# Seven products for eight on more K tiles of a chain of projections, and a feed forward in four parts

## The chip, the cores and the metric

The kernel runs on one core of a Trainium2 chip, in one launch. The metric is the device time of that core in microseconds, lower is better.

## The reference

Three layers on 256 tokens of width 2048, all in float32: two hybrid layers (chunked band attention, gated linear attention, attention to a memory, output projection, layer norm) and one block with a recurrent mixer, a forgetting attention, gates and a feed forward. What the change touches are dense products of the third block:

```python
proj = h @ w_in                        # its gate columns g_a and g_b, 2048 each
merged = jax.nn.sigmoid(g_a) * y_a + jax.nn.sigmoid(g_b) * y_b
x = x + rms_norm(merged @ w_o, norm_mix_post)
h = rms_norm(x, norm_ffn_pre)
gate, up = jnp.split(h @ w_ffn_in, 2, axis=-1)          # 5632 columns each
x = x + rms_norm((jax.nn.silu(gate) * up) @ w_ffn_down, norm_ffn_post)
```

## The kernel before

The kernel is a list of jobs. A job multiplies 256 tokens (two halves of 128) by 512 columns of a weight, over K tiles of 128 rows. Weights come from HBM in tiles of 512 KB (two K tiles by 512 columns) on SyncE's queue. Each is split into two float32r parts, a high one on ScalarE and the rest on VectorE (lines 356, 357, and 506, 507 for the shared jobs), and `three` (lines 439 to 443) multiplies with three matmuls of 512 columns: high by high, high by low, low by high. A tile of weights ("part") so costs 12 matmuls, for both halves of the tokens. All scratch is 41 slots of 512 KB (`N_SLOT`), for raw weights, split weights, hidden rows and sums alike.

`run` walks over the parts in order. `ahead` (line 370) loads up to four raw tiles and splits up to `N_HL` = 6 parts in front of the one that TensorE is told to run, as far as slots are free. Work of other stages (attention heads, recurrence, hidden groups) waits in generators that `pump` steps when they are due by an estimated clock, or that a consumer drains.

`Shared` (line 79) is two jobs with the same activations, a (gate) and b (up). For a quad of four K tiles they form a product of 2 by 2 blocks on each side: the two halves of the tokens by the two pairs of K tiles, and the two pairs of K tiles by the two jobs. Eight block products would be needed; seven do, with sums of blocks as operands (c, d, a, T1, T2, T3 and T4, each with 6 matmuls). Sums of the activations are made once per quad (`combos_of`, line 616, on GpSimd and VectorE). Sums of the weights are made in place for every pair by accumulating transfers between slots, which GpSimd issues (`add`, line 303; `sums`, line 317): after the split of "a" it issues a += b, b += d and d += a, and after that of "c" it issues c += d. T1 is the split of a, T2 of d, T3 of b and T4 of c, as they then stand. TensorE runs plain parts, d and c first, then a, T1, T2, T4, T3 into four PSUM banks and the two main tiles; ScalarE and VectorE combine them (lines 462 and 483 to 497).

In the feed forward (from line 1784) 11 groups of 512 hidden columns are done in parts of 4, 4 and 3. The first group is two single jobs; the other ten are shared pairs with one quad, K tiles 12 to 15. After a part's groups come four single jobs for `w_ffn_down`, whose sums over the parts are kept in four slots (`post_part`, line 1768; `residual_jobs`, line 1614, for the last part and for `w_o`). `hidden` (line 1742) turns a finished pair into the rows that the down jobs read; a job that needs them earlier drains it (line 1760).

Of the kernel before, what the change touches and what calls it, by code (L numbers as in the profile page):

```python
# [12 lines left out]
ALU = mybir.AluOpType  # L13
# [45 lines left out]
class Job:  # L59
# [72 lines left out]
class Builder:  # L132
# [116 lines left out]
    def run(self, jobs, loaded_first, split_first):  # L249
# [283 lines left out]
def network(ctx, tc, a):  # L533
# [82 lines left out]
    def combos_of(get2, quad):  # L616

        xi, ci = B.alloc(2)
        x, c = v4(xi), s(ci).rearrange("p (n k t) -> p n k t", n=4, k=2)
        for k in (0, 2):  # L620
            both = get2(quad[k])
            G.tensor_tensor(x[:, k:k + 2], both[:, :, 0, :].bitcast(F32), both[:, :, 1, :].bitcast(F32), ALU.add)
        x11, x21, x12, x22 = (x[:, k:k + 2, t * P:t * P + P] for k in (0, 2) for t in (0, 1))
        G.tensor_tensor(c[:, 0], x22, x21, ALU.subtract)
        G.tensor_tensor(c[:, 2], x11, x21, ALU.subtract)
        V.scalar_tensor_tensor(c[:, 1], c[:, 0], -1.0, x11, ALU.mult, ALU.subtract)
        G.tensor_tensor(c[:, 3], x12, c[:, 1], ALU.add)
        ids = B.alloc(2, F32R)
        B.split_to(s(ids[0]), s(ids[1]), s(ci))
        B.release([xi, ci])  # L630
        return ids

    def parted(ids):
        return tuple(s(i).rearrange("p (n k t) -> p n k t", n=4, k=2) for i in ids)
# [849 lines left out]

    def start_f(g):
        B.drain([gens["bf"]])
        st[f"yb{g}"] = B.alloc(2, F32R)
        fm = s(st["fm"])

# [37 lines left out]
    def post_gate(key, c):  # L1527
# [4 lines left out]
                A.activation(vt(st[f"{key}{c}"])[:, t, :], ps[:, t, :], AF.Tanh, scale=rs2h[:, t:t + 1])  # L1532
        return post

    def post_upb(c):
# [29 lines left out]

    merging = {}

    def merged(c):
# [4 lines left out]
        B.release([st[f"gb{c}"]])  # L1573

    def merged_get(kt):
        gen = merging.pop(kt // 4, None)
# [6 lines left out]
    for g in range(2):  # L1583
# [10 lines left out]
            X(6144 + 512 * g, 512, act, keep_rows(st, f"bv{g}"))  # L1594
        W(5120 + 512 * g, act, keep_scaled(st, f"bk{g}"))
        W(4096 + 512 * g, act, keep_scaled(st, f"bq{g}", SCALE, then=lambda g=g: start_f(g)))
    for c in range(4):
        X(9224 + 512 * c, 512, act, post_gate("gb", c))
# [4 lines left out]
    for c in range(3):  # L1603
        X(7176 + 512 * c, 512, act, post_gate("ga", c))
    for g in range(2):
        W(3072 + 512 * g, act, post_ag(g))
    X(7176 + 512 * 3, 512, act, post_gate("ga", 3))
# [3 lines left out]
                        pre=B.settle if c == 0 else None))  # L1611


    def residual_jobs(label, w_, post_row, resid, done, act_, order, k0=0, partial=None, pre1=None):

        q = {}

# [29 lines left out]
        def finish(t):  # L1647
# [9 lines left out]
        for c in range(4):  # L1657
            jobs.append(Job("x", w_, 512 * c, 512, act_, post(c), order=order, k0=k0,
                            pre={0: begin, 1: pre1, 2: load_x}.get(c), apart=(label, n - 4 if c == 2 else 0, n) if c > 1 else None))

    fact = row_act(lambda: B.release(xsrc["ids"]))
    f = {"h": []}
# [1 line left out]
    def mix_done(ids, t):  # L1664
        if t == 0:
            xsrc["ids"] = B.alloc(4)

        def rows(c):
            return vt(ids[c])[:, t, :]

        for c in range(4):
            eng = V if c % 2 == 0 else G
            eng.tensor_tensor(vt(xsrc["ids"][c])[:, t, :], rows(c), f["wb"](c), ALU.mult)

        f[t] = rows
        if t == 0:
            B.start(feeder(fact, 0, F0, FG))
        else:
            def done():
                B.release(ids + f["wi"])  # L1680
                f["make"] = make_fcombos()
                B.start(f["make"])
            start_late(fact, [f[0], f[1]], x1res, None, done, False)

    def pre_w2():
# [1 line left out]
        f["wb"] = bcast(a["norm_ffn_pre_2"][0], f["wi"])  # L1687

    residual_jobs("o", a["w_o_2"][0], a["norm_mix_post_2"][0], tokens(xres), mix_done, Act(merged_get), range(NKT),
                  pre1=pre_w2)  # L1690


    wf = a["w_ffn_in_2"][0]
# [23 lines left out]
            B.start(f[("gen", c)])  # L1717
        return post

    QUADS = [(12, 13, 14, 15)]  # L1720

    def make_fcombos():
        for quad in QUADS:
            f.setdefault("combos", []).append(combos_of(lambda k: B.act[:, k:k + 2], quad))
            yield 3000

    def fcombos(q):
        if f["make"] in B.side:
            B.drain([f["make"]])
        return parted(f["combos"][q])  # L1730

    def post_both(c):

        def post(gi, ui):
# [1 line left out]
            B.start(f[("gen", c)])  # L1736
            f["units"] = f.get("units", 1) + 1
            if f["units"] * 512 == D_FF:
                B.release(sum(f["combos"], []))
        return post  # L1740

    def hidden(c, gi, ui=None):
# [15 lines left out]
        B.release([gi])  # L1758

    def hidden_get(kt):  # L1760
        gen = f.pop(("gen", kt // 4), None)
# [3 lines left out]

    hact = Act(hidden_get)

    def post_part(c, new):
        def post(ps):
            if c == 0 and new:  # L1770
                f["part"] = B.alloc(4)
            p = s(f["part"][c])
            if new:
                V.tensor_copy(p, flat(ps))
            else:
                V.tensor_tensor(p, p, flat(ps), ALU.add)
        return post

    def out_done(ids, t):
        for c in range(4):  # L1780
# [1 line left out]
            eng.dma_start(a["out"][0, t * P:(t + 1) * P, c * 512:(c + 1) * 512], vt(ids[c])[:, t, :])  # L1782

    at = 0
    for g, n in enumerate((4, 4, 3)):
        for c in range(n):
            c0 = 512 * (at + c)
            head = (g, c) == (0, 0)
            if not head:
                std = range(16 - 4 * len(QUADS))  # L1790
                gate = Job("x", wf, c0, 512, fact, lambda ps: None, order=std, open=(1,))
                up = Job("x", wf, D_FF + c0, 512, fact, lambda ps: None, order=std)
                jobs.append(Shared(gate, up, QUADS, fact, fcombos, post_both(c)))
                continue
            jobs.append(Job("x", wf, c0, 512, fact, first_gate if head else post_gate2, apart=("ffn", 0, 8) if head else None))
            jobs.append(Job("x", wf, D_FF + c0, 512, fact, first_up if head else post_up2(c), apart=("ffn", 0, 4) if head else None))
        order, k0 = range(4 * n), 4 * at
        if g < 2:
            for c in range(4):
                jobs.append(Job("x", a["w_ffn_down_2"][0], 512 * c, 512, hact, post_part(c, g == 0), order=order, k0=k0))  # L1800
        else:
            residual_jobs("down", a["w_ffn_down_2"][0], a["norm_ffn_post_2"][0], tokens(x1res), out_done, hact, order, k0,
                          partial=lambda: f["part"])
        at += n

    B.run(jobs, load_b, lambda: (split_b(), B.release([mem_in.pop(0)])))
# [52 lines left out]
```

## Time and profile before

| | |
|---|---|
| median of 3 runs | 2400.83 us (2399.18 to 2401.85) |
| profiled execution | 2401.03 us; span from first to last instruction 2399.3 us |
| TensorE busy | 2380.5 us, 99% of the span |
| VectorE, ScalarE, GpSimd busy | 65%, 48%, 18% |
| granted TensorE clock, mean | 0.998 |
| accumulating transfers | 40 of 512 KB, median 7.2 us from issue to landing |

A busy share is that of the whole span; which engine a stretch waits for is read from the timelines of that stretch. A matmul's own duration in the trace overlaps with the next one's, so the price of one is the distance between starts.

### The profile page before, as it was taken

The numbers are of one execution on the slowest core, as the hardware profiler recorded it, in microseconds if no ns is written. First come the engines' busy times: TensorE is split into PE (matmuls) and PEld (weight loads), VectorE is DVE, ScalarE is ACT, GpSimd is POOL, SyncE is SP. The second block draws the span as 40 slices with busy tenths as digits, with TensorE's granted clock in tenths as the row PEclk, the third lists the DMA queues.
The fourth block names the chain that finished last, engine by engine and source line by source line (L and its number), as shares of the span: only waits on it lengthen the run. The fifth ranks groups of instructions, "written<-read, shape, count | busy, mean of one in ns | idle before, by whom it ended". The sixth has DMA issues, their size and how long they took to land. (4 is left out here: it accounts for less than half of the span.)

```text
span 2399.3 us, 31682 instructions
## 1 busy us (share of the span) xinstructions
PE 2380.5 (99%) x12045; PEld 2005.0 (84%) x12045; DVE 1566.2 (65%) x1783; ACT 1160.0 (48%) x1553; POOL 441.5 (18%) x646
## 2 busy tenths in 40 slices
PE   9999999999999999999999999999999999999998
PEld 7888888888888888888888888888888888888876
DVE  6587567566865667766775655657567557665675
ACT  5444455345454553655554434445555445544553
POOL 0330010004400110354754440001100000000000
PEclk9999999999999999999999999999999999999999
DMA  9545567674556574944654556675877578767773
GB/s 329 184 147 187 167 188 261 205 244 141 176 167 187 189 256 148 295 154 128 193 160 151 199 185 193 196 243 171 274 229 224 190 209 261 228 215 226 223 241 131
DMA packets 319672, 485.62 MB, mean 202 GB/s; under 512 B 22600, under 2 KB 162208, under 8 KB 319520
## 3 DMA queue, kind: packets, MB, share of 16 engines
q1 hardware_dynamic: 312528, 459.48, 58.8%
q0 software_dynamic: 6400, 23.07, 4.9%
q8 instruction: 94, 1.54, 0.3%
q10 hardware_dynamic: 592, 1.06, 0.1%
q14 instruction: 58, 0.48, 0.1%
HBM read 454.18 MB, written 8.40 MB: 193 GB/s over the span
## 5 line engine op out<-in xcount | busy, mean ns | idle before, releaser
L357 DVE TENSOR_TENSOR slot<-slot,slot 128x1024 fp32r<-128x1024 f32 x770 | 967.0, 1292 | 266.6 <-ACT slot L356 253.0
L356 ACT CAST slot<-slot 128x1024 fp32r<-128x1024 f32 x770 | 774.4, 1047 | 299.8 <-PE main L442 94.5
L428 PE MATMUL main<-act,slot 128*128 128x512 f32 x1824 | 651.2, 400 | 0.0
L441 PE MATMUL main<-slot,act 128*128 128x512 f32 x1488 | 589.5, 396 | 0.7 <-ACT slot L356 0.7
L442 PE MATMUL main<-slot,act 128*128 128x512 f32 x1488 | 580.0, 390 | 1.6 <-DVE slot L357 1.6
L443 PE MATMUL main<-slot,act 128*128 128x512 f32 x1488 | 580.3, 390 | 0.0
L429 PE MATMUL main<-act,slot 128*128 128x256 f32 x1824 | 510.0, 280 | 0.0
L428 PEld LDWEIGHTS main<-act,slot 128*128 128x128 f32 x1824 | 342.5, 188 | 80.3 <-issue 1.1
L429 PEld LDWEIGHTS main<-act,slot 128*128 128x128 f32 x1824 | 344.2, 189 | 0.8
L443 PEld LDWEIGHTS main<-slot,act 128*128 128x128 f32 x1488 | 279.3, 188 | 59.2
L442 PEld LDWEIGHTS main<-slot,act 128*128 128x128 f32 x1488 | 279.7, 188 | 58.3 <-DVE slot L357 2.8
L441 PEld LDWEIGHTS main<-slot,act 128*128 128x128 f32 x1488 | 279.6, 188 | 57.3 <-ACT slot L356 1.1
L441 PE MATMUL main<-slot,slot 128*128 128x512 f32 x620 | 244.2, 394 | 0.7 <-ACT slot L506 0.7
L443 PE MATMUL main<-slot,slot 128*128 128x512 f32 x620 | 242.6, 391 | 0.0
L442 PE MATMUL main<-slot,slot 128*128 128x512 f32 x620 | 242.1, 390 | 0.0
L304 POOL DMA_DIRECT2D slot<-slot x40 | 35.0, 874 | 563.4 <-DMA slot<-in_w_ffn_in_dram 196.8
L443 PEld LDWEIGHTS main<-slot,slot 128*128 128x128 f32 x620 | 116.8, 188 | 25.8 <-DVE slot L507 1.3
L441 PEld LDWEIGHTS main<-slot,slot 128*128 128x128 f32 x620 | 116.9, 188 | 25.3 <-ACT slot L506 1.4
L442 PEld LDWEIGHTS main<-slot,slot 128*128 128x128 f32 x620 | 116.8, 188 | 23.4
L507 DVE TENSOR_TENSOR slot<-slot,slot 128x1024 fp32r<-128x1024 f32 (+1 forms) x91 | 98.6, 1102 | 33.5 <-ACT slot L506 33.5
L846 POOL TENSOR_TENSOR slot<-slot 128x128 f32<-128x128 f32 x144 | 79.2, 581 | 192.3 <-PE main L428 93.2
L506 ACT CAST slot<-slot 128x1024 fp32r<-128x1024 f32 (+1 forms) x91 | 85.1, 956 | 47.0 <-DMA slot<-slot 16.5
(225 smaller groups left out, 1987.0 us busy)
## 6 DMA issues: line engine op xcount, KB each, us to landing
slot<-in_w_in_dram SPq DMA_DIRECT2D x384, 512.0 KB, 3.8
slot<-in_w_ffn_in_dram SPq DMA_DIRECT2D x176, 512.0 KB, 4.9
slot<-in_w_ffn_down_dram SPq DMA_DIRECT2D x88, 512.0 KB, 4.8
slot<-in_w_out_dram SPq DMA_DIRECT2D x64, 512.0 KB, 4.8
slot<-slot POOLq DMA_DIRECT2D x40, 512.0 KB, 7.2
slot<-in_w_o_dram SPq DMA_DIRECT2D x32, 512.0 KB, 4.7
slot<-in_w_mem_kv_dram SPq DMA_DIRECT2D x31, 512.0 KB, 6.4
slot<-in_w_up_b_dram SPq DMA_DIRECT2D x16, 512.0 KB, 4.6
```

The source lines that it names most:

```text
L304: nc.gpsimd.dma_start(self.s(out), self.s(x), accum_op=ALU.add)
L356: nc.scalar.copy(h, src)
L357: nc.vector.tensor_tensor(l, src, h.bitcast(F32), ALU.subtract)
L428: nc.tensor.matmul(job.ps[:, f, :], h[:, k, fs], xs, start=st, stop=False)
L429: nc.tensor.matmul(job.ps[:, f, :S], l[:, k, fs], xh, start=False, stop=en)
L441: nc.tensor.matmul(o, xh, h, start=start, stop=False)
L442: nc.tensor.matmul(o, xh, l, start=False, stop=False)
L443: nc.tensor.matmul(o, xl, h, start=False, stop=stop)
L506: nc.scalar.copy(h, src)
L507: nc.vector.tensor_tensor(l, src, h.bitcast(F32), ALU.subtract)
L846: G.tensor_tensor(view(E[:, l, :]), view(bt), ref, ALU.subtract)
```

## The change

Seven products for eight are used on more K tiles. Gate and up pairs have two quads, K tiles 8 to 11 and 12 to 15, where they had one. The down jobs of all parts but the last become two shared pairs each, with the first four K tiles of the part as a quad. The output projection's first two jobs become a pair with one quad, the last two stay. Of the eight gate jobs, four become two pairs with one quad. The last part's first two down jobs run interleaved, without a quad.

The feed forward runs in parts of 3, 3, 3 and 2 groups. In `Shared.sequence` the last two plain parts of both jobs move behind c, and a pair with two quads has one part less of look-ahead (`tight`). A class `Combos` makes the activations' sums in a generator, started when their rows are there.

```diff
-        self.apart, self.open = apart or (None, 0, 0), open
+        self.apart, self.open, self.tight = apart or (None, 0, 0), open, 0
...
-        rest = slice(2, None)
-        seq = own(self.b, slice(0, 1)) + mine("d") + own(self.b, slice(1, 2)) + mine("a") + own(self.b, rest)
-        seq += own(self.a, slice(0, 1)) + mine("c") + own(self.a, slice(1, None))
+        seq = own(self.b, slice(0, 1)) + mine("d") + own(self.b, slice(1, 2)) + mine("a") + own(self.b, slice(2, -2))
+        seq += own(self.a, slice(0, 1)) + mine("c") + own(self.a, slice(1, -2))
+        seq += own(self.b, slice(-2, None)) + own(self.a, slice(-2, None))
...
+        for x in (self, a, b):
+            x.tight = int(len(self.quads) > 1)
...
+            cap -= job.tight
             cap += sum(parts[j][0].kind == "s" and parts[j][1][0] == "a" for j in hls)
...
+    class Combos:
+        def start(self):
+            def gen():
+                for quad in self.quads:
+                    self.ids.append(combos_of(self.get2, quad))
+                    yield 3000
...
+    def shared_pair(w_, cs, act_, order, combos, post, pres=(None, None), k0=0):
+        std = [k for k in order if k not in sum(combos.quads, ())]
+        ja, jb = (Job("x", w_, c, 512, act_, lambda ps: None, order=std, k0=k0, pre=pre, open=op)
+                  for c, pre, op in zip(cs, pres, ((1,), ())))
+        return Shared(ja, jb, combos.quads, act_, combos, post)
...
+    jobs.append(shared_pair(w, (9224 + 512 * 2, 9224 + 512 * 3), act, range(NKT), gcombos, post_gates("gb", 2, False)))
...
+    jobs.append(shared_pair(w, (7176 + 512 * 0, 7176 + 512 * 1), act, range(NKT), gcombos, post_gates("ga", 0, True)))
...
+        if combos:
+            jobs.append(shared_pair(w_, (0, 512), act_, order, combos, both, (pre1, begin), k0))
+        else:
+            one, two = (Job("x", w_, 512 * c, 512, act_, post(c), order=order, k0=k0, pre=pre)
+                        for c, pre in ((0, pre1), (1, begin)))
+            jobs.append(Shared(one, two, [], act_, None, None))
...
-    QUADS = [(12, 13, 14, 15)]
...
+    fcombos = Combos(lambda k: B.act[:, k:k + 2], (8, 9, 10, 11), (12, 13, 14, 15))
...
-    for g, n in enumerate((4, 4, 3)):
+    for g, n in enumerate((3, 3, 3, 2)):
...
-        if g < 2:
-            for c in range(4):
-                jobs.append(Job("x", a["w_ffn_down_2"][0], 512 * c, 512, hact, post_part(c, g == 0), order=order, k0=k0))
+        if g < 3:
+            for c in (0, 2):
+                jobs.append(shared_pair(a["w_ffn_down_2"][0], (512 * c, 512 * c + 512), hact, order, Hidden(),
+                                        post_parts(c, g == 0), k0=k0))
```

## Rows read from the trace of the kernel before

**Rows 1.** The page: the span, and busy time, share and instructions of each engine.
```profile
span 2399.3 us, 31682 instructions
...
PE 2380.5 (99%) x12045; PEld 2005.0 (84%) x12045; DVE 1566.2 (65%) x1783; ACT 1160.0 (48%) x1553; POOL 441.5 (18%) x646
```

**Rows 2.** Timeline of TensorE: start, duration (us), line, out<-in; bank products of two pairs.
```profile
2008.20 0.39 PE L441 MATMUL bank<-slot,act 128*128 128x512 f32 x1
...
2015.00 0.39 PE L441 MATMUL main<-slot,act 128*128 128x512 f32 x1
...
2051.33 0.39 PE L441 MATMUL bank<-slot,act 128*128 128x512 f32 x1
...
2055.41 0.39 PE L441 MATMUL main<-slot,act 128*128 128x512 f32 x1
```

**Rows 3.** Stretches: us, busy us of each engine, granted clock, DMA share, GB/s.
```profile
2015.00:2058.00 43.00, 43.00 (x195) 35.60 (x194) 31.53 (x34) 24.05 (x29) 3.48 (x4) 1.00 0.83 246
2333.49:2337.35 3.86, 3.86 (x9) 2.78 (x10) 2.50 (x3) 1.38 (x2) 0.00 (x0) 0.56 0.54 201
```

**Rows 4.** Timeline of GpSimd: issues of adds, and what ended the idle time before.
```profile
2016.59 0.87 POOL L304 DMA_DIRECT2D slot<-slot  x1 [18.73 <-DMA slot<-in_w_ffn_in_dram]
2021.84 0.87 POOL L304 DMA_DIRECT2D slot<-slot  x1 [4.38 <-DMA slot<-slot]
2030.75 0.87 POOL L304 DMA_DIRECT2D slot<-slot  x1 [8.03 <-DMA slot<-slot]
2039.44 0.87 POOL L304 DMA_DIRECT2D slot<-slot  x1 [7.83 <-issue]
2059.42 0.87 POOL L304 DMA_DIRECT2D slot<-slot  x1 [19.11 <-DMA slot<-in_w_ffn_in_dram]
2064.58 0.90 POOL L304 DMA_DIRECT2D slot<-slot  x1 [4.29 <-DMA slot<-slot]
...
2238.78 0.87 POOL L304 DMA_DIRECT2D slot<-slot  x1 [4.73 <-issue]
2249.13 0.87 POOL L304 DMA_DIRECT2D slot<-slot  x1 [9.48 <-DMA slot<-slot]
```

**Rows 5.** Timeline of ScalarE: two splits behind the last add of a pair.
```profile
2045.12 2.00 ACT L506 CAST slot<-slot 128x1024 fp32r<-128x1024 f32 x2 [1.20 <-DMA slot<-slot]
```

**Rows 6.** The page's groups: VectorE's half of a split; busy, mean ns, idle before.
```profile
L357 DVE TENSOR_TENSOR slot<-slot,slot 128x1024 fp32r<-128x1024 f32 x770 | 967.0, 1292 | 266.6 <-ACT slot L356 253.0
```

**Rows 7.** Timeline of VectorE: first and last of the five additions behind T3.
```profile
2018.18 0.68 DVE L493 TENSOR_TENSOR slot<-bank,slot 128x512 f32<-128x512 f32 x1
...
2020.70 0.68 DVE L497 TENSOR_TENSOR slot<-slot,slot 128x512 f32<-128x512 f32 x1
```

**Rows 8.** Timeline of TensorE: the wait before the last part's hidden group.
```profile
2330.82 0.33 PE L529 MATMUL bank<-ident,slot 128*128 128x128 f32 x1 [1.39 <-DVE slot L1750]
2332.27 0.99 PE L529 MATMUL bank<-ident,slot 128*128 128x128 f32 x7 [1.12 <-DVE slot L1750]
2333.49 0.50 PE L441 MATMUL main<-slot,slot 128*128 128x512 f32 x1 [0.24 <-ACT slot L506]
...
2336.94 0.57 PE L443 MATMUL main<-slot,slot 128*128 128x512 f32 x1
2337.35 0.40 PE L441 MATMUL main<-slot,slot 128*128 128x512 f32 x1
```

**Rows 9.** Timeline of TensorE: the same place in the first part of four groups.
```profile
1857.33 1.03 PE L529 MATMUL bank<-ident,slot 128*128 128x128 f32 x8
1858.61 0.50 PE L441 MATMUL main<-slot,slot 128*128 128x512 f32 x1 [0.24 <-ACT slot L506]
```

**Rows 10.** Stretch of the gate jobs, columns as in rows 3.
```profile
1270.00:1320.00 50.00, 50.00 (x251) 42.22 (x251) 30.09 (x46) 25.70 (x41) 22.71 (x52) 1.00 0.51 160
```

**Rows 11.** The page: the software queue; issues of adds, KB each, us to landing.
```profile
q0 software_dynamic: 6400, 23.07, 4.9%
...
slot<-slot POOLq DMA_DIRECT2D x40, 512.0 KB, 7.2
```

More of the change, by code (lines that the diff above doesn't have):

```diff
@@ L631, in combos_of, with __init__, __call__, release @@
         return ids
+    class Combos:
+        def __init__(self, get2, *quads):
+            self.get2, self.quads, self.ids = get2, quads, []
+        def start(self):
[3 more added lines that the diff above has]
+                    yield 3000
+            self.gen = gen()
+            B.start(self.gen)
+        def __call__(self, q):
+            if self.gen in B.side:
+                B.drain([self.gen])
+            return parted(self.ids[q])
+        def release(self):
+            B.release(sum(self.ids, []))
+    def shared_pair(w_, cs, act_, order, combos, post, pres=(None, None), k0=0):
[3 more added lines that the diff above has]
+        return Shared(ja, jb, combos.quads, act_, combos, post)
     def parted(ids):
@@ L1486, in start_f @@
         B.drain([gens["bf"]])
+        if g == 1:
+            gcombos.start()
         st[f"yb{g}"] = B.alloc(2, F32R)
@@ L1533, in post_gate, with post_gates, post @@
         return post
+    gcombos = Combos(lambda k: B.act[:, k:k + 2], (12, 13, 14, 15))
+    def post_gates(key, c, last):
+        def post(*ids):
+            for e, i in enumerate(ids):
+                st[f"{key}{c + e}"] = i
+                for t in range(2):
+                    A.activation(vt(i)[:, t, :], vt(i)[:, t, :], AF.Tanh, scale=rs2h[:, t:t + 1])
+            if last:
+                gcombos.release()
+        return post
     def post_upb(c):
@@ L1566, in network @@
     merging = {}
+    FIRST = (0, 1, 2, 3)
+    ocombos = Combos(lambda k: B.act[:, k:k + 2], FIRST)
     def merged(c):
@@ L1573, in merged @@
         B.release([st[f"gb{c}"]])
+        if c == 1:
+            ocombos.start()
     def merged_get(kt):
@@ L1602, in network @@
                         pre=(lambda: B.drain(gens["f0"] + gens["f1"])) if c == 0 else None))
-    for c in range(3):
-        X(7176 + 512 * c, 512, act, post_gate("ga", c))
+    jobs.append(shared_pair(w, (7176 + 512 * 0, 7176 + 512 * 1), act, range(NKT), gcombos, post_gates("ga", 0, True)))
+    X(7176 + 512 * 2, 512, act, post_gate("ga", 2))
     for g in range(2):
@@ L1611, in network, with residual_jobs @@
                         pre=B.settle if c == 0 else None))
-    def residual_jobs(label, w_, post_row, resid, done, act_, order, k0=0, partial=None, pre1=None):
+    def residual_jobs(label, w_, post_row, resid, done, act_, order, combos, k0=0, partial=None, pre1=None):
         q = {}
@@ L1654, in finish, with both @@
             done(q["r"], t)
-        n = len(order) // 2
-        for c in range(4):
+        def both(i0, i1):
+            for c, i in enumerate((i0, i1)):
+                post(c)(vt(i))
+            B.release([i0, i1])
+            combos.release()
+        n = len(order) // 2
+        if combos:
[4 more added lines that the diff above has]
+            jobs.append(Shared(one, two, [], act_, None, None))
+        for c in (2, 3):
             jobs.append(Job("x", w_, 512 * c, 512, act_, post(c), order=order, k0=k0,
-                            pre={0: begin, 1: pre1, 2: load_x}.get(c), apart=(label, n - 4 if c == 2 else 0, n) if c > 1 else None))
+                            pre=load_x if c == 2 else None, apart=(label, n - 4 if c == 2 else 0, n)))
     fact = row_act(lambda: B.release(xsrc["ids"]))
@@ L1680, in done @@
                 B.release(ids + f["wi"])
-                f["make"] = make_fcombos()
-                B.start(f["make"])
+                fcombos.start()
             start_late(fact, [f[0], f[1]], x1res, None, done, False)
@@ L1718, in post_up2 @@
         return post
-    QUADS = [(12, 13, 14, 15)]
[L1722 to L1730, printed above, removed]
+    fcombos = Combos(lambda k: B.act[:, k:k + 2], (8, 9, 10, 11), (12, 13, 14, 15))
+    hcombos = []
     def post_both(c):
@@ L1738, in post @@
             if f["units"] * 512 == D_FF:
-                B.release(sum(f["combos"], []))
+                fcombos.release()
         return post
@@ L1758, in hidden @@
         B.release([gi])
+        if c == 1 and f.setdefault("groups", 0) < 3:
+            f["groups"] += 1
+            hcombos.append(Combos(lambda k: kx(f["h"][k // 2]), FIRST))
+            hcombos[-1].start()
     def hidden_get(kt):
@@ L1766, in network, with post_parts, post, __call__ @@
     hact = Act(hidden_get)
[L1768 to L1776, printed above, removed]
-        return post
+    def post_parts(c, new):
+        def post(*ids):
+            for e, i in enumerate(ids):
+                if new:
+                    f.setdefault("part", {})[c + e] = i
+                else:
+                    V.tensor_tensor(s(f["part"][c + e]), s(f["part"][c + e]), s(i), ALU.add)
+                    B.release([i])
+            if c == 2:
+                hcombos.pop().release()
+        return post
+    class Hidden:
+        quads = (FIRST,)
+        def __call__(self, q):
+            return hcombos[-1](q)
     def out_done(ids, t):
@@ L1789, in network @@
             if not head:
[L1790 to L1793, printed above, removed]
+                jobs.append(shared_pair(wf, (c0, D_FF + c0), fact, range(NKT), fcombos, post_both(c)))
                 continue
@@ L1797, in network @@
         order, k0 = range(4 * n), 4 * at
-        if g < 2:
-            for c in range(4):
-                jobs.append(Job("x", a["w_ffn_down_2"][0], 512 * c, 512, hact, post_part(c, g == 0), order=order, k0=k0))
-        else:
-            residual_jobs("down", a["w_ffn_down_2"][0], a["norm_ffn_post_2"][0], tokens(x1res), out_done, hact, order, k0,
-                          partial=lambda: f["part"])
+        if g < 3:
+            for c in (0, 2):
+                jobs.append(shared_pair(a["w_ffn_down_2"][0], (512 * c, 512 * c + 512), hact, order, Hidden(),
+                                        post_parts(c, g == 0), k0=k0))
+        else:
+            residual_jobs("down", a["w_ffn_down_2"][0], a["norm_ffn_post_2"][0], tokens(x1res), out_done, hact, order, None, k0,
+                          partial=lambda: [f["part"][c] for c in range(4)])
         at += n
```

5 lines of the change are left out of this document (3 added, 2 removed).

## Prediction

> **What bounds the kernel now.** I read the busy times first: TensorE is busy for 2380.5 of 2399.3 us, every other engine for 65% or less [rows 1]. So a product taken away is time gained, if nothing comes late for the rest. Then the price of a product, from TensorE's timeline: from 2008.20 to 2015.00 a gate and up pair runs its last five products (a, T1, T2, T4, T3), 30 matmuls of 512 columns, without an idle gap: 6.80 / 30 = 0.227 us each [rows 2]. One pair ends at 2015.00 and the next pair's first bank product comes at 2051.33, 43.13 after the last one: 186 matmuls x 0.227 = 42.2 and 0.9 of transposes. The granted clock is 1.00 there, the level of 2.4 GHz [rows 3]. Third, what else a pair needs by its end: the four accumulating transfers on GpSimd's queue (line 304) and the splits that read what they leave. They are what the change doubles, so their chain gets most of the working.
>
> **The chain of adds as it is.** GpSimd issues an add only once the one before has landed. In the pair that begins at 2015.00 the issues stand at 2016.59, 2021.84, 2030.75 and 2039.44: 5.25, 8.91 and 8.69 apart, 22.85 in all (mean 7.6) [rows 4]. ScalarE's split that waits for the last add starts at 2045.12, 5.7 after its issue [rows 5]; this is T4's (T1 and T2 stand ahead of it, T3 behind). TensorE comes to T4 at 2055.41 [rows 2]. So the chain ends about 9 us before it is needed, split included: it is hidden, with that much slack and no more. The spread of one interval over the feed forward goes from 5.16 (2059.42 to 2064.58) to 10.35 (2238.78 to 2249.13) [rows 4].
>
> **The change, part by part.**
> *Products removed.* A quad of four K tiles on a pair costs 48 matmuls as plain products and 42 as seven. There are 10 quads before. After there are 20 on gate and up, 6 on the down parts (three parts, two pairs), 1 on the output projection and 2 on the gate pairs: 19 more. 19 x 6 = 114 matmuls x 0.227 = **-25.8 us**, all on TensorE's path [rows 2]. Other parts (3, 3, 3, 2 for 4, 4, 3) leave the number of products as it is.
> *Work added beside.* Each new quad needs seven splits for four: 57 more at 1.29 on VectorE [rows 6] and 1.0 on ScalarE [rows 5]. VectorE has 31.5 busy us in a pair of 43 [rows 3]; a gate and up pair gets 3 more splits, 35.4 of 41.7. The new combinations of the activations go on GpSimd behind the adds of their pair. I cost all that at nothing; the products cover it, and without cover each split is 1.29 us.
> *Adds: gate and up, the term that decides.* A pair now has eight. The order in which they go on GpSimd's queue is three of the first quad, three of the second, then one for each c. So c's add of the first quad, the one T4 of that quad reads, stands behind six adds where it stood behind three. Reckoned from the pair's start:
> - First add: +1.6 before (2016.59 against 2015.00) [rows 2, 4]. The split of "a" that it follows is now one half part later in the pair and the look-ahead is one part shorter, 2 x 1.36 = 2.7, so +4.3; if VectorE also puts it behind T3's five additions (2018.18 to 2021.38) [rows 7], +6.4 at most. I take +5.
> - Then 5.2, 9.3 (8.91 and a little, for a busier queue), 0.9 for the issue of the second quad's first add, which waits for no add, 7.6, 7.6, and 0.9: c's add at 5 + 31.5 = +36.5. Its split starts 5.7 later and ScalarE's half takes 1.0 [rows 5]: +43.2.
> - TensorE's turn for that T4: eight plain parts of 12 matmuls, four half parts (d and c, twice) of 6, and a, T1, T2 with 18: 138 x 0.227 = 31.3, and 0.9 of transposes: +32.2.
> It waits 11 us. A wait of 1.4 and 1.1 us on this kernel was followed by nine matmuls about 0.43 apart (2333.49 to 2337.35), 1.8 us more than at 0.227 [rows 8]; the granted clock is 0.56 over them, nearly all of it at the level of 1.2 GHz [rows 3]. One such stretch per wait. So 12.8, say **13 us in each of ten pairs, +130**. Bounds: with every interval 5.2 and the first add at +4.3, the split is ready at +33.6, a wait of 1.4; with every interval 10.35 and +6.4, at +56.3, a wait of 24. I stand near the mean interval, because the transfers share the engines with as many loads as before. The second quad's c add comes about 8 us after the first's, and TensorE reaches that T4 6.8 us after the first: no further wait of size. What is queued behind: ScalarE and VectorE take splits in order, so the next pair's first parts, and with them its first add, shift by the same wait. It is not made good later.
> *Adds: down.* One quad, 12 K tiles: T4's turn comes after 126 matmuls, +28.6. The chain as before: first add +1.6 to +3, 22.85, 5.7 and 1.0 give +31 to +32.6: 3 us late. With the slower matmuls 5 in each second pair, and 2 in each first, which has a wait of its own (next): 3 x 5 + 3 x 2 = **+21**, bounds 0 and 60.
> *Feed forward parts.* The last hidden group of a part was needed 72 matmuls (16.3 us) into the next job where the part had four groups: a wait of 0.24 there [rows 9]. With two plain groups ahead (48 matmuls, 10.9 us) the waits at the end were 1.4, 1.1 and 0.24 and then the slow clock [rows 8]. Now b, d, b, a, c, a come first: 60 matmuls, 13.6 us. In between: 2 us x 3 parts, **+6**, bounds 0 and 13. The last part keeps 10.9.
> *Gate pairs and output projection.* One quad in 16 K tiles has the shape of today's pairs, and keeps their 9 us of slack. On the gate pairs GpSimd is busy 22.71 of 50 us with the recurrence heads [rows 10], between whose blocks the adds now stand. **+5**, bounds -3 and +25.
> *Slots.* There are 41. Beside the two quads' eight raw tiles and two parked "a" splits, 16 to 18 hold combinations, hidden rows and partial sums; loads and splits have about 12. I cost it at nothing.
> Sum, on the profiled execution (span 2399.3, 2401.03 us in all, 0.2 over the median 2400.83): 2401 - 25.8 + 130 + 21 + 6 + 5 = 2537, **2540 us**.
>
> **A rule against these rows.** The rows have packets wait: the shortest step from add to add is 5.16 us and the median add lands 7.2 after issue [rows 4, 11]. The Trainium skill's page "DMA: Bandwidth & Descriptors" (Anatomy of one DMA — SWDGE (gpsimd) path) fits a GpSimd-issued transfer as 2.0 us and its bytes at 436 GB/s, which for 512 KB would be an estimated 3.2 us, and its section on queues, rings and completion order has each engine go round the queues packet by packet. By that c's add would be issued near +20 and nothing would wait. No row of this trace has an add so short, and the measurement decides.
>
> **Rivals.**
> 1. *The chain stays hidden: faster.* Decided by one interval: 5 + 4x + 1.8 + 5.7 + 1.0 is below 32.2 as long as x is under 4.7 us, or 5.5 if the first add still goes at +1.6. The rows have 5.16 and 5.25 for steps with no loads about [rows 4], which speaks for it; the two steps behind them are 8.7 to 9.6. Then 2401 - 25.8 + 6 = **2381**. This is also where the Trainium skill's rule just named would put the time. Chance 0.15.
> 2. *The transfers' bytes bound the pair, not their chain.* The engines' share in 2015 to 2058 is 0.83: 35.7 us [rows 3]. The software queue took 4.9% of 2399 us for 23.07 MB [rows 11], 2.67 us for 512 KB; four more adds are 10.7. Together 46.4 for a pair against 41.7 of products; then ten pairs at 46.4 for 43.1 are +33, and the 54 matmuls saved elsewhere -12: **2422**, slower by 0.9%. Against it: the chain is longer than that. Chance 0.08.
> 3. *Slots run out.* If fewer than two parts are ahead, each of the pair's parts waits for its own load and split; a pair of 65 us would give 2401 - 12 + 219 + 27 = **2635**. For it: the count above. Against it: the parts are smaller by one group just for that room. Chance 0.07.
>
> **How the numbers follow.** Forecast 0.70, rivals 0.15, 0.08 and 0.07. The forecast alone runs from 2440 to 2650 (a wait of 4 to 22 per pair); with rival 2's near side and rival 3, 2410 to 2680 holds about 8 in 10. A difference of 0.2% is what the runs can tell from none. Slower: the forecast and rival 3 whole and most of rival 2, 0.81; within 0.2%: 0.04; faster: 0.15.
>
> **What would show it.** After the change: 116 adds for 40; matmuls down by 114; the first bank products of neighbouring pairs 54 to 56 us apart for 43.1; in each pair an idle gap on TensorE ahead of the first quad's T4, with ScalarE's split there ended by an add's landing; GpSimd's issues 5 to 9 apart almost without a break; granted clock at the lower level after each gap. If the pairs are 41.7 apart, the chain was hidden and I am wrong in sign; if the gap is spread over the plain parts with loads as releasers, it is slots or bytes.

## The result, and the profile after

The changed kernel takes 2657.47 us (median of 4 runs, 2651.64 to 2658.83) against 2401.06 us for the kernel before beside it: a ratio of 1.1065, 95% interval 1.1045 to 1.1084. It is 256 us slower, where the likeliest case was 139 us slower (2540), in a range up to 2680.

The page of the changed kernel, its span, busy times, software queue, the groups of adds and their landing (compare rows 1 and 11):

```profile
span 2656.3 us, 32017 instructions
...
PE 2425.1 (91%) x11931; PEld 2017.0 (76%) x11931; DVE 1695.6 (64%) x1924; ACT 1240.2 (47%) x1661; POOL 543.5 (20%) x752
...
q0 software_dynamic: 17344, 62.92, 12.4%
...
L308 POOL DMA_DIRECT2D slot<-slot x116 | 102.1, 921 | 773.0 <-DMA slot<-slot 389.4
...
slot<-slot POOLq DMA_DIRECT2D x116, 512.0 KB, 5.9
```

TensorE has 114 matmuls fewer and is no longer busy all the time: 231 us of the span are idle, where there were 19 [rows 1]. There are 116 adds for 40, and of the 773.0 us that GpSimd is idle in front of one, 389.4 are a wait for the landing of the one before. The lines have moved: `three` is now lines 446 to 448, the splits of the shared jobs 511 (ScalarE) and 512 (VectorE), plain splits 360 and 361, the add 308.

The waits of TensorE and ScalarE, summed by what they wait for (total us, times, longest):

```profile
PE main L446 <- ACT slot L511: 134.2, 16, 12.3
PE main L446 <- ACT slot L360: 25.7, 7, 10.6
...
ACT slot L511 <- DMA slot<-slot: 295.1, 35, 17.0
```

The first row is TensorE waiting for a ScalarE split. Ten of its 16 waits are the first quad's T4 in the ten gate and up pairs, 9.5 to 12.3 us each and 111 in all; three of 6.4 to 7.5 us are hidden groups at the ends of parts. The last row says what ScalarE's splits waited for: the landing of an accumulating transfer.

One pair, on TensorE, ScalarE and GpSimd (timelines: start, duration, line, form, idle time before and its releaser). The pair before it ends at 2014.57.

```profile
2046.82 0.39 PE L448 MATMUL bank<-slot,slot 128*128 128x512 f32 x1
2059.24 0.80 PE L446 MATMUL main<-slot,act 128*128 128x512 f32 x1 [12.03 <-ACT slot L511]
2060.50 0.79 PE L447 MATMUL main<-slot,act 128*128 128x512 f32 x1 [0.47 <-DVE slot L512]
```
```profile
2058.14 1.04 ACT L511 CAST slot<-slot 128x1024 fp32r<-128x1024 f32 x1 [14.48 <-DMA slot<-slot]
```
```profile
2021.27 0.87 POOL L308 DMA_DIRECT2D slot<-slot  x1 [22.93 <-DVE slot L512]
2027.62 0.87 POOL L308 DMA_DIRECT2D slot<-slot  x1 [5.49 <-DMA slot<-slot]
2036.99 1.77 POOL L308 DMA_DIRECT2D slot<-slot  x2 [8.50 <-DMA slot<-slot]
2045.41 0.87 POOL L308 DMA_DIRECT2D slot<-slot  x1 [6.64 <-DMA slot<-slot]
2050.88 1.77 POOL L308 DMA_DIRECT2D slot<-slot  x2 [4.60 <-DMA slot<-slot]
2056.04 0.87 POOL L308 DMA_DIRECT2D slot<-slot  x1 [3.39 <-DMA slot<-slot]
```

Read them together. The second issue of the group at 2050.88 is c's add of the first quad, some 37 us after the pair began. It lands as the idle time of ScalarE's split ends, at 2058.14, and T4 goes at 2059.24. TensorE was ready at 2047.05. The first bank products of neighbouring pairs stand 54.9, 56.5, 58.2, 56.2, 58.2 and 54.6 us apart, mean 56.4, against 43.1 before [rows 2].

### The profile page after: what moved, and what is told of

Its sections match the earlier page's. It is cut to its first block, busy times and chain, and to the rows that moved or that the text cites. A ratio compares the mean times of both kernels' runs of the same rounds, so it can differ in the third digit from the quotient of the medians.

```text
span 2656.3 us, 32017 instructions
## 1 busy us (share of the span) xinstructions
PE 2425.1 (91%) x11931; PEld 2017.0 (76%) x11931; DVE 1695.6 (64%) x1924; ACT 1240.2 (47%) x1661; POOL 543.5 (20%) x752
## 5 line engine op out<-in xcount | busy, mean ns | idle before, releaser
L361 DVE TENSOR_TENSOR slot<-slot,slot 128x1024 fp32r<-128x1024 f32 (+1 forms) x694 | 885.0, 1308 | 266.7 <-ACT slot L360 259.9
L360 ACT CAST slot<-slot 128x1024 fp32r<-128x1024 f32 (+1 forms) x694 | 700.0, 1046 | 276.5 <-DVE slot L361 75.5
L446 PE MATMUL main<-slot,act 128*128 128x512 f32 x1332 | 541.7, 407 | 138.0 <-ACT slot L511 112.2
L447 PE MATMUL main<-slot,act 128*128 128x512 f32 x1332 | 534.7, 401 | 18.3 <-DVE slot L361 12.4
L448 PE MATMUL main<-slot,act 128*128 128x512 f32 x1332 | 530.7, 398 | 0.0
L512 DVE TENSOR_TENSOR slot<-slot,slot 128x1024 fp32r<-128x1024 f32 (+1 forms) x230 | 268.5, 1191 | 305.6 <-ACT slot L511 304.1
L446 PEld LDWEIGHTS main<-slot,act 128*128 128x128 f32 x1332 | 256.8, 193 | 197.4 <-ACT slot L511 117.2
L511 ACT CAST slot<-slot 128x1024 fp32r<-128x1024 f32 (+1 forms) x230 | 224.9, 1012 | 341.3 <-DMA slot<-slot 295.1
L447 PEld LDWEIGHTS main<-slot,act 128*128 128x128 f32 x1332 | 256.8, 193 | 81.9 <-DVE slot L361 19.8
L448 PEld LDWEIGHTS main<-slot,act 128*128 128x128 f32 x1332 | 257.0, 193 | 54.0
L308 POOL DMA_DIRECT2D slot<-slot x116 | 102.1, 921 | 773.0 <-DMA slot<-slot 389.4
L446 PE MATMUL main<-slot,slot 128*128 128x512 f32 x586 | 235.3, 402 | 22.0 <-ACT slot L511 22.0
L447 PE MATMUL main<-slot,slot 128*128 128x512 f32 x586 | 232.7, 397 | 8.5 <-DVE slot L361 6.2
L448 PE MATMUL main<-slot,slot 128*128 128x512 f32 x586 | 232.3, 396 | 0.5 <-DVE slot L512 0.5
L446 PEld LDWEIGHTS main<-slot,slot 128*128 128x128 f32 x586 | 112.5, 192 | 47.2 <-ACT slot L511 24.5
L447 PEld LDWEIGHTS main<-slot,slot 128*128 128x128 f32 x586 | 112.7, 192 | 33.3 <-DVE slot L361 7.4
L448 PEld LDWEIGHTS main<-slot,slot 128*128 128x128 f32 x586 | 112.2, 192 | 26.5 <-DVE slot L512 2.9
```

The source lines that it names most:

```text
L308: nc.gpsimd.dma_start(self.s(out), self.s(x), accum_op=ALU.add)
L360: nc.scalar.copy(h, src)
L361: nc.vector.tensor_tensor(l, src, h.bitcast(F32), ALU.subtract)
L446: nc.tensor.matmul(o, xh, h, start=start, stop=False)
L447: nc.tensor.matmul(o, xh, l, start=False, stop=False)
L448: nc.tensor.matmul(o, xl, h, start=False, stop=stop)
```

## The experiments

In the diffs the lines are those of the changed kernel. "Distance" is that between the first bank products of neighbouring gate and up pairs.

**The adds left out.** Does the loss hang on them at all?

```diff
-            nc.gpsimd.dma_start(self.s(out), self.s(x), accum_op=ALU.add)
+            pass
```

> Leaves out every accumulating transfer (the sums of weights are not formed; T1 to T4 multiply the plain tiles), everything else as in the changed kernel. Theory (chain, and engines' queues behind it): no split waits for a landing, no recurrence head stands behind an add: 2401 - 26 and some 10 to 20 us for hidden groups needed earlier, 2385 to 2395 us. Rival (slots and look-ahead): waits stay where they are, above 2500 us. The rival of the bytes expects the same as the theory here.

Measured 2428.27 us (2427.78 to 2429.41), ratio 1.0116 [1.0101, 1.0131]. The distance is 42.2, where the products alone are 41.7, and no pair has a gap of size, with the same 41 slots:

```profile
1910.70:1953.00 42.30, 42.13 (x190) 34.53 (x189) 33.79 (x35) 25.83 (x29) 0.00 (x0) 1.00 0.61 199
```

(Columns as in rows 3.) So the adds are worth 2657 - 2428 = 229 us. But the time is not the 2385 to 2395 expected: 53 us lie above 2401 - 25.8 = 2375 with no add in the kernel. Two places hold them. In the gate stage TensorE waits ten times for a split, up to 3.3 us each. And at each part's end the way from the last pair's first bank product to the first down pair's takes 45.9, 47.9 and 48.7 us, where its 168 matmuls and the transposes need 39. Why is to be seen on VectorE there:

```profile
2004.07 2.43 DVE L512 TENSOR_TENSOR slot<-slot,slot 128x1024 fp32r<-128x1024 f32 x2
...
2018.52 4.63 DVE L361 TENSOR_TENSOR slot<-slot,slot 128x1024 fp32r<-128x1024 f32 x4
2023.95 1.23 DVE L361 TENSOR_TENSOR slot<-slot,slot 128x1024 fp32r<-128x1024 f32 x1 [0.81 <-ACT slot L360]
2025.10 0.75 DVE L1805 SCALAR_TENSOR_TENSOR slot<-slot,rs,tz 128x512 f32<-128x512 f32 x1
2025.88 0.75 DVE L1806 SCALAR_TENSOR_TENSOR slot<-slot,rs,slot 128x512 f32<-128x512 f32 x1
```

From 2004.07 to 2023.15 it runs splits and quad sums without a pause, and only then the two products that finish the hidden group. TensorE wanted them at 2024.2 and starts its transposes at 2026.69.

**The same without the gate pairs**, to place the rest of the 53 us.

> No accumulating transfers (the sums of weights are left out, the splits read what the loads brought) and the gate jobs single; the rest as changed. With all adds gone the kernel still took 2428.3, 53 us more than its own products would give (2401 less 25.8). Theory: of these some 22 lie in the gate stage (its first up product came 18.9 us later than before, with 12 products less), from the splits of the pairs between the recurrence heads; so this run is at 2428.3 - 18.9 = 2409, range 2404 to 2416. Rival: the gate stage's delay is taken up later, or the loss lies in the feed forward: 2420 to 2431.

Measured 2406.97 us (2405.59 to 2409.75), ratio 1.0029 [1.0017, 1.0041]: as the theory has it. The gate pairs cost 21 us net, 24 with their 12 products, before any add. What is left, 2407 - (2401 - 25.8 + 2.7) = 29, is the sum of the excesses at the part ends: 45.9 + 47.9 + 48.7 - 3 x 39 = 25.5, and two starts of a part 1.7 late.

**One quad on gate and up**, the rest as changed.

```diff
-    fcombos = Combos(lambda k: B.act[:, k:k + 2], (8, 9, 10, 11), (12, 13, 14, 15))
+    fcombos = Combos(lambda k: B.act[:, k:k + 2], (12, 13, 14, 15))
```

> Gate and up have one quad again (K tiles 12 to 15); parts of 3, 3, 3, 2 groups, down, output projection and gate pairs as changed. Theory: with four adds per pair and T4 at +40 the chain is hidden again, pairs 43.1 us apart for 58: 2657 - 10 x 15 = 2507 us (2490 to 2530). Rival (the smaller parts and the new order of parts make the pairs slow): pairs stay above 50 us, 2580 us or more.

Measured 2484.50 us (2480.80 to 2485.51), ratio 1.0346 [1.0330, 1.0361]. Inside a part every distance is back at 43.1, with TensorE busy throughout. The gain of 173 (187 with the 60 products that come back, 13.6) is more than was expected and more than the gaps inside the pairs: the second quad also delays what follows a part's last pair.

**Gate jobs single.**

```diff
-    jobs.append(shared_pair(w, (9224 + 512 * 2, 9224 + 512 * 3), act, range(NKT), gcombos, post_gates("gb", 2, False)))
+    X(9224 + 512 * 2, 512, act, post_gate("gb", 2))
+    X(9224 + 512 * 3, 512, act, post_gate("gb", 3))
...
-    jobs.append(shared_pair(w, (7176 + 512 * 0, 7176 + 512 * 1), act, range(NKT), gcombos, post_gates("ga", 0, True)))
+    X(7176 + 512 * 0, 512, act, post_gate("ga", 0))
+    X(7176 + 512 * 1, 512, act, post_gate("ga", 1))
```

> The two gate pairs are four single jobs again, as in the kernel before; all else as changed. Theory (adds in GpSimd's queue hold up the recurrence heads behind them, and ScalarE's splits stand behind those heads): the 43 us that the gate stage lost come back less 12 products' time, 2657 - 46 = 2611 us (2600 to 2625). Rival (the gate stage lost its time to TensorE work of the heads, which only moved there): it comes up elsewhere, 2640 to 2660 us.

Measured 2613.84 us (2612.51 to 2616.89), ratio 1.0890 [1.0874, 1.0906], as expected: 44 us, 46 with the products. The mechanism is in the changed kernel's rows of that stage, on GpSimd, ScalarE and TensorE:

```profile
1308.51 0.85 POOL L308 DMA_DIRECT2D slot<-slot  x1 [5.36 <-DMA slot<-slot]
1309.09 2.49 POOL L880 TENSOR_TENSOR slot<-slot 128x128 f32<-128x128 f32 x6
...
1312.08 0.69 POOL L890 TENSOR_SCALAR slot<-slot 128x64 f32<-128x64 f32 x1
```
```profile
1312.81 1.06 ACT L891 ACTIVATE slot<-slot 128x1024 f32<-128x1024 f32 x1 [13.10 <-POOL slot L890]
1313.90 1.06 ACT L892 ACTIVATE slot<-slot 128x1024 f32<-128x1024 f32 x1
1314.86 1.03 ACT L360 CAST slot<-slot 128x1024 fp32r<-128x1024 f32 x1
```
```profile
1304.31 1.05 PE L530 MATMUL bank<-slot 128*128 128x128 f32 x8
1315.94 0.80 PE L446 MATMUL main<-slot,act 128*128 128x512 f32 x1 [10.58 <-ACT slot L360]
```

An add at the head of GpSimd's queue waits for the one before it to land. Behind it stands the recurrence head's work (lines 880 to 890), behind that an activation on ScalarE that waits 13.10 us, and behind that the split of the next weights.

**Down jobs single** in the first three parts.

```diff
-            for c in (0, 2):
-                jobs.append(shared_pair(a["w_ffn_down_2"][0], (512 * c, 512 * c + 512), hact, order, Hidden(),
-                                        post_parts(c, g == 0), k0=k0))
+            for c in range(4):
+                jobs.append(Job("x", a["w_ffn_down_2"][0], 512 * c, 512, hact, post_single(c, g == 0), order=order, k0=k0))
```

> The down jobs of the first three parts are four single jobs again; everything else as changed. Theory (T splits that wait for an add stand on ScalarE ahead of the last hidden group's): the 84 us of a down part go back to the 65 of its products plus a few: 2657 - 3 x 17 = 2606 us (2590 to 2620). Rival (the down parts are late because the hidden rows come from pairs with eight adds): the wait stays, 2640 us or more.

Measured 2577.01 us (2570.38 to 2585.38), ratio 1.0736 [1.0711, 1.0761]: 80 us where 51 were expected, or 89 with the 36 products that come back (8.2). The rows of the changed kernel at a part's end, TensorE and ScalarE:

```profile
2147.79 0.39 PE L448 MATMUL main<-slot,slot 128*128 128x512 f32 x1
2150.22 0.33 PE L534 MATMUL bank<-ident,slot 128*128 128x128 f32 x1 [2.04 <-DVE slot L1806]
2151.67 1.75 PE L534 MATMUL bank<-ident,slot 128*128 128x128 f32 x7 [1.12 <-DVE slot L1806]
2160.09 0.79 PE L446 MATMUL main<-slot,slot 128*128 128x512 f32 x1 [6.66 <-ACT slot L511]
```
```profile
2158.50 1.04 ACT L511 CAST slot<-slot 128x1024 fp32r<-128x1024 f32 x1 [8.88 <-DMA slot<-slot]
2159.45 1.07 ACT L511 CAST slot<-bank 128x512 fp32r<-128x512 f32 x2
```

The hidden group's own split (from the bank, 2159.45) had its input by about 2153.4. It stands behind T2's split, and that waits 8.88 us for an add. An in-order engine hands the add's lateness to a product that has nothing to do with it.

**Adds of both quads issued in turn**: a += b for both, then b += d for both, then d += a for both, so that each quad's chain has the other's issue in its waiting time.

```diff
-                add(a, b)
-                add(b, d)
-                add(d, a)
+                if q < len(job.quads) - 1:
+                    return
...
+                for a, b, d in sets:
+                    add(a, b)
+                for a, b, d in sets:
+                    add(b, d)
+                for a, b, d in sets:
+                    add(d, a)
```

> The same 116 accumulating transfers and the same bytes; on a pair with two quads GpSimd issues them quad by quad in turn (a of both, b of both, d of both, then c of both), so each waits for one issued two places earlier. Theory (the chain of landings sets T4 of the first quad): c's add is issued some 8 us earlier in the pair, the wait of about 12 us per gate and up pair falls to 1 to 5 us, ten pairs, so 2560 us (2530 to 2590) for 2657. Rival (the bytes of the transfers bound the pair) and rival (slots and look-ahead bound it): the same work and the same slots, 2657 within 20 us.

Measured 2605.20 us (2602.73 to 2607.70), ratio 1.0852 [1.0836, 1.0868]. It fell between the two: half the gain that the theory gave. Distances are 50.2 to 52.8. The first and the last issue of one pair, of eight:

```profile
2004.80 0.87 POOL L308 DMA_DIRECT2D slot<-slot  x1 [22.61 <-DVE slot L519]
...
2033.86 0.87 POOL L308 DMA_DIRECT2D slot<-slot  x1 [3.09 <-DMA slot<-in_w_ffn_in_dram]
```

Eight adds now take 29.1 us from first to last issue, where they took 34.8. Order on the queue is part of the cost, but the chain still ends too late. Beside it, the median add now lands 7.6 us after issue where it was 5.9, and 15 issues in the feed forward wait for loads, as the last one here does (55.7 us in all).

**The bytes without the chain.** 108 transfers of the same size and kind go to a tile that nobody reads. The sums are left out, the gate jobs are single, and the number of attention heads that run side by side differs, so only the feed forward is compared.

```diff
-            nc.gpsimd.dma_start(self.s(out), self.s(x), accum_op=ALU.add)
+            src = self.act[:, 0:2].rearrange("p k j t -> p (k j t)").bitcast(F32)
+            nc.gpsimd.dma_start(self.scratch, src, accum_op=ALU.add)
```

> As many transfers of the same size at the same places in GpSimd's queue, but between rows of the activations and a scratch tile that no product reads; each still waits for the one before. The sums of weights are left out (T1 to T4 multiply the plain tiles); the gate jobs are single ones, and fewer attention and recurrence heads run at a time to make room for the scratch tile, so only the feed forward is compared: from its first gate sigmoid to the end 916 us in the changed kernel, 713 without any add, 704 in the kernel before. Theory (what costs is that splits wait for the landings): 715 to 760 us there. Rival (the bytes of the adds crowd out the loads): above 850 us.

The whole took 2560.94 us in one run. From its first gate group's sigmoid to the end the feed forward took 807 us, between theory and rival, so as a total it decides nothing. Inside a part it does:

```profile
1982.90:2025.10 42.20, 42.03 (x189) 34.49 (x188) 34.84 (x37) 26.75 (x31) 4.32 (x5) 1.00 0.94 273
2025.10:2067.40 42.30, 42.13 (x190) 34.54 (x189) 35.17 (x37) 26.62 (x31) 5.16 (x6) 1.00 0.94 273
```

The pairs run 42.2 us apart with the DMA engines at 0.94, more than in the changed kernel (0.83 and 0.82 in 1986.5 to 2043 and 2043 to 2101.1), and TensorE waits for nothing. Five or six adds go through in that time, not eight: here too each waits for the one before, and a backlog grows. Eight would make 12.6 MB with the pair's 16 loads, by estimate 46 us at these 273 GB/s; so the bytes may set a floor near 46, below the 56.4 of the changed kernel, and no run tests it. The rest of the 807 us is lost where the sums of the activations stand behind that backlog on GpSimd (lines are 3 further down here; waits, as above):

```profile
ACT slot L514 <- POOL slot L635: 112.0, 6, 35.8
```

**The sums of weights computed on GpSimd**, without a DMA.

```diff
-            nc.gpsimd.dma_start(self.s(out), self.s(x), accum_op=ALU.add)
+            nc.gpsimd.tensor_tensor(self.s(out), self.s(out), self.s(x), ALU.add)
```

> The sums of weights are formed by GpSimd itself (an addition of 128x1024, 2.4 us where this kernel has one), in the same place and order, in place of accumulating transfers: no landing to wait for. Theory: c's sum of the first quad is ready some 22 us into the pair where it was ready at 43, ahead of TensorE's turn at 32; the heads wait 2.4 us per sum and not 6 to 9. 2380 to 2420 us. Rival (slots and look-ahead): little changes, above 2550 us. If GpSimd's additions slow VectorE's splits beside them, 2420 to 2500 us.

Measured 2627.02 us (2626.08 to 2630.92), ratio 1.0948 [1.0929, 1.0966]: in the rival's range, but by the mechanism of the third case, larger than expected there. The DMA engines fell to 0.43 in 1990 to 2050 and the time hardly moved. That doesn't clear the bytes, since another engine is late now, VectorE; the groups of GpSimd and VectorE in 1990 to 2380, and a stretch of both timelines:

```profile
L308 POOL TENSOR_TENSOR slot<-slot,slot 128x1024 f32<-128x1024 f32 x51 | 152.9, 3008 | 220.9 <-DVE slot L512 218.8
L361 DVE TENSOR_TENSOR slot<-slot,slot 128x1024 fp32r<-128x1024 f32 x57 | 96.5, 1715 | 9.6 <-ACT slot L360 7.1 <-ACT slot L511 1.2
```
```profile
2050.23 2.35 DVE L512 TENSOR_TENSOR slot<-slot,slot 128x1024 fp32r<-128x1024 f32 x2
2052.50 3.39 DVE L361 TENSOR_TENSOR slot<-slot,slot 128x1024 fp32r<-128x1024 f32 x1
2055.81 6.72 DVE L512 TENSOR_TENSOR slot<-slot,slot 128x1024 fp32r<-128x1024 f32 x2
```
```profile
2051.58 16.54 POOL L308 TENSOR_TENSOR slot<-slot,slot 128x1024 f32<-128x1024 f32 x5 [35.62 <-DVE slot L512]
```

A split that takes 1.2 us (2.35 for two at 2050.23) takes 3.4 beside GpSimd's additions. VectorE is busy 51.41 of 60 us in 1990 to 2050, against 34.34 in the changed kernel.

**A shorter chain**: adds in turn, c += d on VectorE, gate jobs single.

> Three edits: adds of the two quads issued in turn, as in the run that did only that (2605); c += d by VectorE right behind the split of d that it waits for anyway, so GpSimd's chain is three adds long and T4 waits for nothing of its own; gate jobs single. Theory: d of the first quad lands about 24 us into the pair, ahead of T2's turn at 30, the pairs come to 42 to 46 us: 2614 - 130 - 20 for shorter chains in the down pairs = 2465 us (2430 to 2500). Rival (bytes): the pairs stay at 50, 2550 us or more.

Measured 2543.28 us (2541.03 to 2545.69), ratio 1.0594 [1.0576, 1.0612]: well above the theory and just below the rival's range. T4's long wait is gone, and TensorE's largest waits are smaller and many (lines are 8 further down here: 368 and 369 the plain splits, 519 and 520 the others):

```profile
PE main L454 <- ACT slot L519: 28.0, 14, 6.8
PE main L455 <- DVE slot L369: 19.9, 13, 3.1
PE bank L542 <- DVE slot L1814: 16.7, 8, 5.4
PE main L454 <- ACT slot L368: 14.1, 9, 4.8
...
ACT slot L368 <- DMA slot<-in_w_ffn_in_dram: 65.0, 33, 5.6
```

Distances stay at 50 to 52.3, as the rival of the bytes had it, though the DMA engines are at 0.81 in one such pair (1975.1 to 2027.4). Now plain splits wait for loads (65.0 us, 33 times), and the splits behind them. Raw tiles that wait for adds hold slots longer, which would start loads later; whether that or the transfers' sharing of the engines makes them late was not told apart.

**Only the smaller parts.** One quad on gate and up, gate and down jobs single.

> Gate and up with one quad, gate jobs and down jobs single again; what is left of the change is the feed forward in parts of 3, 3, 3 and 2 groups, the order with the last two plain parts behind c, and one quad on the output projection. Undone one at a time the three were worth 172.5, 43.4 and 80.2 us, 296 together, which would give 2361; that is below the kernel before without its six products, so the prices must overlap (the chains of a pair and of the next down pair share a queue). Theory: 2401 - 1.4 (six products on the output projection) + 6 (three hidden groups at 2 us, as forecast) = 2406, range 2398 to 2412. Rival: the smaller parts and the new order cost something by themselves, which the undoing one by one has hidden: 2420 or more, with waits at the part boundaries.

Measured 2411.38 us (2409.80 to 2412.29), ratio 1.0045 [1.0031, 1.0058], at the upper end of the theory. TensorE has the last part's wait of rows 8 four times, as here:

```profile
2007.54 0.33 PE L534 MATMUL bank<-ident,slot 128*128 128x128 f32 x1 [1.39 <-DVE slot L1806]
2008.99 0.98 PE L534 MATMUL bank<-ident,slot 128*128 128x128 f32 x7 [1.12 <-DVE slot L1806]
```

With the slow matmuls behind it a wait is 1.4 + 1.1 + 0.2 + 1.8 = 4.5 us [rows 8]; three more are 13.6, less 1.4 of products: +12.2, measured +10.8.

**Down pairs where their chain has time.** One quad on gate and up, gate jobs single, parts of 4, 4 and 3 as before; the two full parts keep the down pairs with a quad.

```diff
-    for g, n in enumerate((3, 3, 3, 2)):
+    for g, n in enumerate((4, 4, 3)):
...
-        if g < 3:
+        if g < 2:
```

> Gate and up with one quad, gate jobs single, feed forward in parts of 4, 4 and 3 groups as before, but the down jobs of the first two parts as shared pairs with one quad (K tiles 0 to 3 of 16) and the quad on the output projection kept. Five quads more than before: 30 products, 6.8 us. Theory: with 16 K tiles a down pair has the shape of a one-quad gate and up pair, whose chain of adds ends about 9 us before its use; so the adds are hidden and only the hidden group costs 1 to 2 us per part: 2401 - 6.8 + 3 = 2397, range 2392 to 2404. Rival: with four groups of hidden rows, sums and partial sums the slots don't do and loads or splits come late: 2410 to 2440.

Measured 2389.19 us (2389.00 to 2389.88, 5 runs), ratio 0.9954 [0.9941, 0.9966]: faster than both kernels, and than expected. In a down pair, GpSimd's last add and ScalarE's splits behind it:

```profile
1910.47 0.86 POOL L308 DMA_DIRECT2D slot<-slot  x1 [7.69 <-issue]
```
```profile
1915.06 2.00 ACT L511 CAST slot<-slot 128x1024 fp32r<-128x1024 f32 x2 [4.06 <-DMA slot<-slot]
```

T4's split is done at 1916.1. TensorE runs that pair's first bank product at 1918.86 and T4 18 matmuls later, near 1922.9: 7 us of slack. Of the 11.4 us gained, 30 products are 6.8. The wait of rows 8 in the last part, 4.5, is gone too, since the last part's first two down jobs now run interleaved and reach the hidden group later.

## Why the prediction was right, and where its sizes were off

The sign, the cause and the place of the largest term were right. That the total stayed in the range was partly luck: the three terms beside T4's wait make 140 us together where 32 were forecast, and each passed its own upper bound (25, 13 and 60), the last narrowly. The range still held the sum because it allowed 22 us per pair, of which the pairs took 14, and reached beyond 2650 only for rival 3, which did not happen. The terms, as forecast and as the runs show them (an undo run's gain with its products added back; distances as listed above; an excess step is what two matmul starts lie further apart than is usual for their kind, summed: 50 us in the gate stage, 1 in that of the kernel before):

| term | forecast | measured | from |
|---|---|---|---|
| products | -25.8 | -25.8 | 114 fewer on the page |
| gate and up, T4's wait in ten pairs | +130 | +142 | mean distance 56.4 - 42.2, times 10 |
| gate stage and output projection | +5 | +46 to +50 | gate jobs single; excess steps in 1290 to 1560 |
| hidden groups at part ends, without adds | +6 | +29 | adds left out, gate jobs single |
| down pairs and part ends, from adds | +21 | +61 to +65 | what is left of 256 |

- **The chain, step by step.** First add: forecast +5, at most +6.4 if it goes behind T3's additions; it went at +6.7 (2021.27 - 2014.57), behind them. c's add: forecast +36.5, measured +37.0. T4's turn: +32.2 and +32.5. T4's split ready: +43.2 forecast; T4 starts at +44.7. The wait was 12.2 for a forecast of 11.
- **The clock behind a wait** was undersized: 1.8 us, taken from a wait of 1.4. Behind the wait of 10.23 us that ends at 2000.94, 15 steps take 7.25 us, 3.8 more than at 0.227, at a granted clock of 0.51, nearly all of it the level of 1.2 GHz. A row behind a short wait didn't carry over to a long one. The stretch, columns as in rows 3:

```profile
2000.94:2008.19 7.25, 6.78 (x15) 4.97 (x16) 6.94 (x7) 6.60 (x8) 0.00 (x0) 0.51 0.41 98
```

- **Gate pairs** failed as a step, not only in size. I gave them the slack of a gate and up pair and put the risk on GpSimd's busy share (22.71 of 50 us). The cost came from the other side: an add that waits at the head of GpSimd's queue stops the recurrence heads, and through them ScalarE's splits. Half of it needs no add at all (24 us with the adds left out). The bound of +25 was too low.
- **Down and hidden groups.** T4's turn in a first down pair was not the place. The hidden group is needed first, and its split stands on ScalarE behind a T split that waits for an add. I priced the two waits apart and missed that one engine's order joins them. The cover that I named for the extra splits, the products, holds inside a part (33.79 busy of 42.3) and fails at its end, where VectorE runs 19 us without a pause.
- **Rival 1**, the chain hidden, fell: from one add to the add that waits for it the pair shown takes 5.2 to 9.4 us, and none in the feed forward under 4.77. The estimate that I drew from the Trainium skill's page, "DMA: Bandwidth & Descriptors" (Anatomy of one DMA — SWDGE (gpsimd) path), 3.2 us, is below all of them; the median landing came 5.9 us after issue.
- **Rival 2**, the bytes, fell as the cause of the 56.4: the engines ran at 0.94 without a wait of TensorE, and with the same 116 adds issued in another order the kernel was 52 us faster. That the bytes lengthen the landings, or hold the pairs at 50 in the two runs with the adds in turn, isn't excluded.
- **Rival 3**, slots, had a near total (2635), but its mechanism isn't that of the gaps: they are single, before T4, and released by an add's landing, and they are gone with the adds left out and the slots as many. That slots play a part in the shortened chain stays open.

The undone parts don't add up: 173.0 + 43.6 + 80.5 = 297, while undoing all three gives 2657.5 - 2411.4 = 246. The surplus of 51 is shared. About half of it lies in the first pairs of the last three parts: with the down jobs single they are 46.7, 45.8 and 47.1 us from the next pair, where they were 56.5, 56.2 and 54.6. So some 28 of the 142 us come with the down pairs ahead of them, and one quad on gate and up removes these too. The rest lies between a part's last pair and the next part's first, where either undo takes away part of the same waits.

## What to carry to other kernels

A chain of dependent transfers is priced from its first possible issue, by the steps that the trace shows, to the turn of what reads it; where the turn comes later, as in the down pairs over 16 K tiles, the same products are a gain. When work that waits is put on an in-order queue, list everything behind it on that queue, and on the queues that those in turn feed: recurrence heads, plain splits and hidden groups paid here for adds that none of them reads. A busy share with room over a whole pair says nothing of the twenty us in which a job ends.

## What the runs showed of the hardware

GpSimd and VectorE slowed each other: beside GpSimd's additions of 128x1024 in float32 (2.4 us at best, 3.0 in the mean) VectorE's split of the same size went from 1.2 to 3.4 us, and the hidden products (line 1805) from 0.75 to 2.4 in the mean. And in two pairs of the run with the bytes alone, the DMA engines at 0.94 with 273 GB/s cost TensorE nothing: no split there waited for one of the adds.
